# A planner that writes a kernel's order learns when each transfer's eighth predecessor ends

## The chip, the cores and the metric

One core of a Trainium2 chip runs the whole kernel in one launch. The metric is the device time of one execution in microseconds (us); every kernel is run several times and the median is quoted.

## The reference, cut to what matters

One decoder layer for a prompt of 1024 tokens and 64 sample tokens (8 sequences of 8), d_model 1024, all in fp32:

```
h = rmsnorm(x) * norm1_g ;  proj = h @ w_in                      # one input projection
y_conv = c_b * conv3(c_c * c_x)                                  # short gated convolution
r,k,v,decay,a,g from the other columns (token shift, low-rank products)
for each token: s = s*decay - (s@kk) (kk*a)^T + v k^T ; y = s@r   # 8 heads of 64
y_rwkv = (groupnorm(y) + bonus) * g
x = x + [y_conv, y_rwkv] @ w_out                                 # output projection
x = x + relu(rmsnorm(x) @ w_ff1)^2 @ w_ff2 ; y = rmsnorm(x)
```

Outputs are y for both kinds of tokens and the new convolution, shift and recurrent states.

## The kernel before

**Matmuls.** Each fp32 operand is split into a high and a low part, and a product is three matmuls (hi*hi, lo*hi, hi*lo). The 1088 tokens are cut into groups of 384, 384 and 320.

**The recurrence.** The 8 heads are taken as 4 pairs, and a pair with a token group is a *unit* (12 units, 0 to 11, three of a pair in a row). Inside a unit the delta rule goes in chunks: within a chunk it is solved with a triangular inverse, from chunk to chunk a state is handed on. This hand-over is the *chain*: 64 steps in all. One step is L1110, L1111 and L1114 on PE (into `rc`), the copy `X` on DVE (L1120), L1122 on PE, `UT` on ACT (L1124), L1126 on PE, then `Gh` on DVE (L1130 or L1132) and `GD` on ACT (L1116), with which the next step's L1114 begins. L1110 and L1111 don't depend on the step before. A unit's result is read out by `py` (L1144) and transposed by `pty` (L1293). Ahead of a unit lie its inverse on POOL (L1040, L1042), the merge of its blocks (`pz` L1074, copies `wz`, `pz` L1082, `Tt` L1086), the transposes `ptk` (L977, copied to `KT` by ACT at L981) and `ptv` (L992, to `VT` at L997), and the bonus `pb` (L953, L954). In the last unit but one, unit 10, chain steps 55 to 60 run; unit 9 has steps 49 to 54.

**The filler.** The matmuls of the input projection (L664, helper `mm_s`) and then of the output projection (L671, helper `mm_m`) need no chain and are laid between the chain's instructions. Their weights come as 256 KB loads `wraw` (L640), issued by ACT except for the first four, and are split by ACT into `whi` (L652) and by DVE into `wlo` (L654).

**Who sets the order.** All streams (chain, inverse, merge, projections, loads, row loads) are Python generators. Before each group of instructions a generator yields `ck(engine, cost, ...)`, with what it needs (`deps`, tiles `acq`). `Weave.run` (from L312) keeps an estimated clock for each engine, always takes the group that can start earliest, and lets its generator emit its instructions. So what the kernel contains is fixed, and the estimated clocks decide only in which order each engine gets it. The engines work through that order one by one; the clocks and costs of the planner exist nowhere on the chip.

**Transfers.** SP and ACT issue them. In the program every transfer is given one of eight semaphores in turn, over both queues, and its issue waits until the transfer eight before it, which had the same semaphore, has ended. The planner before knows nothing of this. The row loads `mr` (`load_row`, L1321) are issued by ACT; they bring rows of the mixed activations for the output projection.

After some 710 us the woven half ends and plain loops follow: the MLP's first product (L103), its second (L1547, L1559) and the final norm.

Of the kernel before, what the change touches and what calls it, by code (L numbers as in the profile page):

```python
# [33 lines left out]
def tile_kernel(ctx: ExitStack, tc: tile.TileContext, io: dict):  # L34
# [105 lines left out]
    def gen_vec():  # L140
# [4 lines left out]
        for nm, ap, n in VECS:  # L145
            SP.dma_start(vr[off[nm]:off[nm] + n, :], ap.rearrange("(m p) -> m p", p=128))
# [13 lines left out]
        SP.dma_start(ssr, io["state_shift"][0].rearrange("b (m p) -> (b m) p", p=128))  # L160
        SP.dma_start(scr, io["state_conv"][0].rearrange("b j (m p) -> (b j m) p", p=128))
# [20 lines left out]
    def gen_masks():  # L182
# [39 lines left out]
        SP.dma_start(unit_d, winit)  # L222
# [39 lines left out]
    class Weave:  # L262
# [41 lines left out]
        def dma(self, kb=192):  # L304

            t = self.charge("SP", 0.5)
            self.clk["DMA"] = max(self.clk["DMA"], t + 0.65) + kb / 360
            return self.clk["DMA"] + 1.05

        def run(self, gens):  # L310

            st = [[0.0, next(g, None), "PE"] for g in gens]  # L312
            while any(a is not None for _, a, _ in st):
                best, held = None, set()
                for i, (r, a, pe) in enumerate(st):
# [10 lines left out]
                    if held.intersection(acq):  # L326
# [3 lines left out]
                            + [self.credits[t][acq.count(t) - 1] + 0.2 for t in acq])  # L330
# [23 lines left out]
    def ck(eng, cost, **o):  # L354
        return eng, cost, o

# [65 lines left out]
    def load_xt(t):  # L422
        s, n = TOK[t]
        xts[t] = p0.tile([128, D], F32, tag="xt", name="xt", bufs=4)
        SP.dma_start(xts[t][:n], tok_rows(io["x_prompt"], io["x_sample"], t))
# [20 lines left out]
    def gen_lora_w():  # L446
        for nm in ("w2", "a2", "g2"):
            yield ck("SP", 1.2 if nm != "g2" else 0.6, deps=[("n1", 2)])
            raw = p0.tile([128, RW], F32, tag="lraw", name="lraw", bufs=2)
            if nm == "g2":  # L450
                SP.dma_start(raw, io[nm][0])
            else:
                SP.dma_start(raw[0:64], io[nm][0])
                SP.dma_start(raw[64:128], io[nm][0])
# [44 lines left out]
    def gen_lora(parts):  # L499

        for p in range(4):
            for g in range(3):
                s, n = GROUPS[g]
                pc = slice(128 * p, 128 * p + 128)
                for nm in parts:
# [22 lines left out]
                    SP.dma_start(dst[pc, s:s + n], t[:, :n])  # L528
# [63 lines left out]
    def post_conv_b(j, g):  # L592
        def f(acc):
# [5 lines left out]
            def store():  # L599
                SP.dma_start(mix_d[128 * j:128 * j + 128, s:s + n], cc[:, s:s + n])  # L600
# [30 lines left out]
    def gen_load(loads):  # L631

        for x, ld in enumerate(loads):
            for i, (pl, t, src) in enumerate(ld.parts):
                if x < 2:
                    yield ck("NO", 0, acq=("wra" + t,))
                else:
                    yield ck("ACT", 0.05, lat=0, acq=("wra" + t,))
                raw = pl["pq"].tile(list(src.shape), F32, tag="wraw" + t, name="wraw", bufs=2)
                (SP if x < 2 else A).dma_start(raw, src)  # L640
# [145 lines left out]
    def load_sgta(u):  # L786
# [4 lines left out]
        SP.dma_start(sg[:, :n], sig_d[pc, s:s + n])  # L791
        ta = at["pe"].tile([128, 384], F32, tag="ta", name="ta")
        SP.dma_start(ta[:, :n], ta_d[pc, s:s + n])
# [32 lines left out]
    def gen_ew(u):  # L826
# [91 lines left out]
        yield ck("SP", 1.9)  # L918
# [3 lines left out]
        for h in range(2):  # L922
            for i in range(2):
                r = 64 * h + 32 * i
                SP.dma_start(lv[h, i], LT[r:r + 32, :nch, 32 * i:32 * i + 32])
# [39 lines left out]
    def gen_tokens(u):  # L965
# [34 lines left out]
        if g == 2:  # L1000
            yield ck("SP", 0.5, nb=True, deps=[("So", p - 1, 4)] if p else [])
            e["Sn"] = Sn = at["pp"].tile([128, NB, 64], F32, tag="Sn", name="Sn")
            SP.dma_start(Sn, io["state_wkv"][0, :, 2 * p:2 * p + 2].rearrange("b h v k -> (h v) b k"))
# [5 lines left out]
    def load_W(u):  # L1009
        Ws[u] = at["pp"].tile([96, 8, 32], F32, tag="W", name="W", bufs=2)  # L1010
        SP.dma_start(Ws[u], unit_d)
        wv.mark(("W", u), wv.dma(96))

    def gen_invert(u):
# [8 lines left out]
        yield ck("SP", 1.6, lat=4.3, deps=[("A", u)])  # L1023
        M, lt_d = at["M"], e["lt_d"]
        for i in range(4):
            SP.dma_start(M[24 * i:24 * i + nb], lt_d[:nb])
# [18 lines left out]
        yield ck("SP", 1.8)  # L1045
        w_d = dp.tile([24, 32, 32], F32, tag="w_d", name="w_d", bufs=3)
        for q in range(4):
            SP.dma_start(w_d[:nb].rearrange("b (m q) t -> q b m t", q=4)[q], W[24 * q:24 * q + nb])
# [3 lines left out]
    def gen_merge(u):  # L1052
# [5 lines left out]
        yield ck("SP", 1.8, lat=6.5, deps=[("w_d", u)] + done(u - 2))  # L1058
# [5 lines left out]
        for h in range(2):  # L1064
            for i in range(2):
                SP.dma_start(Tt[Q[h][i], :nch, Q[h][i]], wv_[h, i])
# [25 lines left out]
    def gen_recur(u):  # L1092
# [53 lines left out]
        if g == 2:  # L1146
# [8 lines left out]
            SP.dma_start(io["new_wkv_p"][0, 0, 2 * p:2 * p + 2].rearrange("h v k -> (h v) k"), So)  # L1155
# [6 lines left out]
    def gen_sample(u):  # L1162
# [3 lines left out]
        def store_s(So, b0):  # L1166
            for b in range(4):
                SP.dma_start(io["new_wkv_s"][0, b0 + b, 2 * p:2 * p + 2].rearrange("h v k -> v h k"),
# [82 lines left out]
    def load_gt(u):  # L1251
# [3 lines left out]
        SP.dma_start(gts[u][:, :n], gate_d[128 * p:128 * p + 128, s:s + n])  # L1255
        wv.dma()

    def gen_finish(u):
# [42 lines left out]
        if p < 3:  # L1301
            def store():
                SP.dma_start(mix_d[512 + 128 * p:640 + 128 * p, s:s + n], gt[:, :n])
# [56 lines left out]
    def load_x(pl, t):  # L1360
        n = TOK[t][1]
        x1[t] = pl.tile([128, D], F32, tag="x1", name="x1", bufs=6 if t < 6 else 3)
        SP.dma_start(x1[t][:n], tok_rows(io["x_prompt"], io["x_sample"], t))
# [68 lines left out]
    def gen_states():  # L1432
# [12 lines left out]
        SP.dma_start(io["new_shift_p"][0, 0].rearrange("(m p) -> m p", p=128), ns[0:14])  # L1445
        SP.dma_start(io["new_shift_s"][0].rearrange("b (m p) -> (b m) p", p=128), ns[14:126])
        SP.dma_start(io["new_conv_p"][0, 0].rearrange("j (m p) -> (j m) p", p=128), ncv[0:8])
        SP.dma_start(io["new_conv_s"][0].rearrange("b j (m p) -> (b j m) p", p=128), ncv[8:72])
# [13 lines left out]
    with tc.manual_schedule():  # L1462
# [3 lines left out]
        SP.dma_start(g1, io["norm1_g"][0].rearrange("(o n) -> o n", o=1))  # L1466
# [63 lines left out]
    def load_f2(ft):  # L1530
        raw = p5.tile([128, D], F32, tag="f2r", name="f2r", bufs=2)
        SP.dma_start(raw, io["w_ff2"][0][128 * ft:128 * ft + 128, :])
# [62 lines left out]
    def final_c(t, pool_too=True):  # L1595
# [11 lines left out]
        SP.dma_start(tok_rows(io["y_prompt"], io["y_sample"], t), out[:n])  # L1607
# [14 lines left out]
    with tc.manual_schedule():  # L1622
# [27 lines left out]
        SP.dma_start(tok_rows(io["y_prompt"], io["y_sample"], seq[-2]), out)  # L1650
# [3 lines left out]
        SP.dma_start(tok_rows(io["y_prompt"], io["y_sample"], last), xg)  # L1654
# [27 lines left out]
```

## Time and profile before

| | |
|---|---|
| runs | 1471.01, 1471.39, 1469.06 us, median 1471.01 |
| profiled execution | 1467.82 us, its span 1466.1 us |
| mean granted TensorE clock | 0.985 of full |
| PE busy | 1428.1 us, 97% |
| ACT busy, DVE busy, POOL busy | 508.4, 823.6, 317.4 us |
| DMA | 108.25 MB, mean 74 GB/s |

The span is the time from the first to the last instruction of the profiled execution; 1.7 us of that execution lie around it. A timeline row gives the start, the duration, the engine (ACTq and SPq are the queues' issuing instructions), the line, the tiles and, in brackets, how long the engine had been idle before and what ended it. Rows of equal form that follow each other are merged (x2, x4), and the duration is then that of all of them.

### The profile page before, as it was taken

To read this page: it belongs to the slowest core of one execution; us is meant where nothing else is said; L and a number is where in the kernel's file an instruction comes from. 1 tells how busy PE (TensorE), PEld (TensorE's weight loads), DVE (VectorE), ACT (ScalarE), POOL (GpSimd) and SP (SyncE) were. 2 spreads that over 40 slices of the span, in tenths; PEclk is the share of its full clock that TensorE was granted. 3 is DMA by queue.
4 is the path that set the end of the run, shared out by engine and by line. 5 is a ranking of instruction groups with operands and counts; after the bars stand their busy time and mean duration, and the time that the engine had idled before them with its cause. 6 is when DMAs were issued, how large, how long until landed. Compare 5 with 4: busy or idle time off the path is not lost.

```text
span 1466.1 us, 25883 instructions
## 1 busy us (share of the span) xinstructions
PE 1428.1 (97%) x10163; PEld 1339.9 (91%) x10163; DVE 823.6 (56%) x1788; ACT 508.4 (35%) x1094; POOL 317.4 (22%) x855
## 2 busy tenths in 40 slices
PE   6999999999989997999999999999999999999997
PEld 5999999998989987999999999999999999999996
DVE  6537767787767785666444344444344344444347
ACT  6532334344333432344522332223322332223315
POOL 4011656654665655000000000000000000000004
PEclk8999999999989998999999999999999999999999
DMA  6242332232232325453210111111111111111103
GB/s 193 94 146 87 80 84 69 66 91 57 72 85 57 74 74 184 149 171 101 87 44 29 58 58 44 42 31 59 44 43 30 58 58 44 42 32 58 36 1 122
DMA packets 140228, 108.25 MB, mean 74 GB/s; under 512 B 43837, under 2 KB 131017, under 8 KB 140106
## 3 DMA queue, kind: packets, MB, share of 16 engines
q1 hardware_dynamic: 65322, 61.29, 14.0%
q10 hardware_dynamic: 74784, 45.30, 10.5%
q8 instruction: 80, 1.31, 0.4%
q14 instruction: 42, 0.34, 0.1%
HBM read 88.46 MB, written 18.09 MB: 73 GB/s over the span
## 4 chain that ended last, share of the span: by engine, by line
PE 87%; DVE 5%; DMA 3%; POOL 2%; issue 1%; ACT 1%; SPq 0%; ACTq 0%; POOLq 0%; DVEq 0%
PE acc L103 24%; PE acc L664 21%; PE acc L1547 17%; PE acc L1559 8%; PE acc L671 6%; DMA mr<-mix_d 1%; PE pm L899 1%; PE py L1144 1%; PE pw L516 1%; PE rc L1122 1%; DMA wraw<-in_w_out 1%; PE rc L1111 1%; PE pt L403 1%; POOL wtmp L1040 1%; POOL W L1042 1%
## 5 line engine op out<-in xcount | busy, mean ns | idle before, releaser
L103 PE MATMUL acc<-h_lo,whi 128*128 128x320 f32 (+1 forms) x720 | 234.8, 326 | 0.0
L103 PE MATMUL acc<-h_hi,wlo 128*128 128x320 f32 (+1 forms) x720 | 234.8, 326 | 0.0
L103 PE MATMUL acc<-h_hi,whi 128*128 128x320 f32 (+1 forms) x720 | 234.7, 326 | 0.0
L664 PE MATMUL acc<-h_hi,whi 128*128 128x384 f32 (+1 forms) x672 | 230.5, 343 | 2.8 <-DVE nsT L259 2.8
L664 PE MATMUL acc<-h_lo,whi 128*128 128x384 f32 (+1 forms) x672 | 229.4, 341 | 1.6 <-DVE h_lo L414 1.6
L664 PE MATMUL acc<-h_hi,wlo 128*128 128x384 f32 (+1 forms) x672 | 229.9, 342 | 0.0
L1549 DVE TENSOR_TENSOR x<-acc,x 128x512 f32<-128x512 f32 (+1 forms) x193 | 132.8, 688 | 124.9 <-PE acc L1547 124.9
L1593 POOL TENSOR_TENSOR rsf<-rsf,nhalf 128x1 f32<-128x1 f32 (+1 forms) x9 | 8.0, 888 | 741.5 <-DVE rsf L1590 740.4
L1425 DVE TENSOR_TENSOR slo<-r,shi 128x384 fp32r<-128x384 f32 (+1 forms) x96 | 51.5, 537 | 204.5 <-ACT shi L1423 204.5
L1040 POOL TENSOR_TENSOR wtmp<-W,gM 96x60 f32<-96x60 f32 (+24 forms) x372 | 122.3, 329 | 155.3 <-DMA gM<-lt_d 71.3
L1547 PE MATMUL acc<-f2h,shi 128*128 128x512 f32 (+1 forms) x386 | 150.2, 389 | 0.0
L1547 PE MATMUL acc<-f2h,slo 128*128 128x512 f32 (+1 forms) x386 | 150.0, 389 | 0.0
L1547 PE MATMUL acc<-f2l,shi 128*128 128x512 f32 (+1 forms) x386 | 149.9, 388 | 0.0
L68 ACT CAST f2h<-f2r 128x1024 fp32r<-128x1024 f32 x32 | 32.0, 1047 | 309.1 <-PE acc L1547 309.1
L103 PEld LDWEIGHTS acc<-h_lo,whi 128*128 128x128 f32 x720 | 135.1, 188 | 0.6
L103 PEld LDWEIGHTS acc<-h_hi,whi 128*128 128x128 f32 x720 | 135.1, 188 | 0.6
L103 PEld LDWEIGHTS acc<-h_hi,wlo 128*128 128x128 f32 x720 | 135.2, 188 | 0.0
L664 PEld LDWEIGHTS acc<-h_hi,whi 128*128 128x128 f32 x672 | 128.6, 191 | 4.5 <-ACT KT L981 3.0
L1042 POOL TENSOR_TENSOR W<-W,wtmp 96x60 f32<-96x60 f32 (+24 forms) x372 | 126.3, 340 | 29.2
L664 PEld LDWEIGHTS acc<-h_lo,whi 128*128 128x128 f32 x672 | 128.7, 191 | 2.7 <-DVE h_lo L414 1.9
L664 PEld LDWEIGHTS acc<-h_hi,wlo 128*128 128x128 f32 x672 | 128.6, 191 | 0.4
L1419 ACT ACTIVATE r<-acc 128x384 f32<-128x384 f32 (+1 forms) x96 | 45.3, 472 | 150.9 <-PE acc L103 141.2
(308 smaller groups left out, 2833.2 us busy)
## 6 DMA issues: line engine op xcount, KB each, us to landing
f2r<-in_w_ff SPq DMA_DIRECT2D x32, 512.0 KB
wraw<-in_w_ff ACTq DMA_DIRECT2D x64, 256.0 KB
wraw<-in_w_in ACTq DMA_DIRECT2D x48, 256.0 KB
wraw<-in_w_out ACTq DMA_DIRECT2D x48, 256.0 KB
xt<-in_x_prompt SPq DMA_DIRECT2D x8, 512.0 KB
x<-in_x_prompt SPq DMA_DIRECT2D x8, 512.0 KB
out_y_prompt<-out SPq DMA_DIRECT2D x7, 512.0 KB
gM<-lt_d SPq DMA_DIRECT2D x32, 96.0 KB
```

Of the source, the lines that this page charges most:

```text
L68: A.copy(hi, src)
L103: PE.matmul(acc[:, :n], a, b, start=(i == 0), stop=(i == 23))
L403: PE.transpose(pt[:, k, :n], xn[:n, 128 * kk:128 * kk + 128], ident[:n, :n])
L664: PE.matmul(acc[:, :n], a, b, start=(k == i == 0), stop=(k == 7 and i == 2))
L671: PE.matmul(acc[:n, :256], a, b, start=(k == i == 0), stop=(k == 7 and i == 2))
L1040: G.tensor_tensor(tv, W[:, 0:nr, r:r + 1].broadcast_to([96, nr, wd]), M[:, r:r + 1, r + 1:32].broadcast_to([96, nr, wd]), op=ALU.mult)
L1042: G.tensor_tensor(W[:, 0:nr, r + 1:32], W[:, 0:nr, r + 1:32], tv, op=ALU.subtract)
L1419: A.activation(r[:, :n], acc[:, :n], AF.Relu)
L1425: V.tensor_tensor(lo, r[:, :n], hi.bitcast(F32), op=ALU.subtract)
L1547: PE.matmul(acc[:, :cn], a, b, start=(j == 0), stop=(j == 3 * FB - 1))
L1549: V.tensor_tensor(x1[t][:, cols], acc[:, :cn], x1[t][:, cols], op=ALU.add)
L1559: PE.matmul(acc[:, :n], a, b, start=(j == 0), stop=(j == 3 * FB - 1))
```

## The change

The planner gets a list `lanes` of the expected end of every transfer so far, eight zeros at first. Each issue of the woven half goes through `sp_dma` or `act_dma`, which appends an expected end of 2.2 us after the planner's now, SP's clock (for SP) or the eighth predecessor's expected end, whichever is last. `dma` and `dma_a`, where the program calls them behind an issue, put their own estimate in its place, and `dma` lets SP's clock wait for the eighth predecessor. A group marked `dma=k` may not start before the expected end of the eighth predecessor of its k-th transfer, plus 0.3 us. Marked are the weight loads on ACT (k=1) and the groups of four small transfers on SP (k=4): stores of `lt_d` and `w_d`, loads of `gM` and `Tt`. The row loads `mr` are counted in the list and are not marked.

```diff
 class Weave:
+            self.lanes = [0.0] * 8
...
         def dma_a(self, kb=192):
             self.clk["DMA"] = max(self.clk["DMA"], self.now + 0.65) + kb / 360
-            return self.clk["DMA"] + 1.05
+            self.lanes[-1] = self.clk["DMA"] + 1.05
+            return self.lanes[-1]
...
         def dma(self, kb=192):
-            t = self.charge("SP", 0.5)
+            t = self.charge("SP", 0.5, self.lanes[-9])
             self.clk["DMA"] = max(self.clk["DMA"], t + 0.65) + kb / 360
-            return self.clk["DMA"] + 1.05
+            self.lanes[-1] = self.clk["DMA"] + 1.05
+            return self.lanes[-1]
...
                     t = max([r + (0.05 if eng == "PE" and pe != "PE" else 0), self.clk[eng]]
                             + [self.done[k] + 0.2 for k in o.get("deps", ())]
-                            + [self.credits[t][acq.count(t) - 1] + 0.2 for t in acq])
+                            + [self.credits[t][acq.count(t) - 1] + 0.2 for t in acq]
+                            + ([self.lanes[o["dma"] - 9] + 0.3] if "dma" in o else []))
...
+    def sp_dma(out, src, **kw):
+        wv.lanes.append(max(wv.now, wv.clk["SP"], wv.lanes[-8]) + 2.2)
+        SP.dma_start(out, src, **kw)
+
+    def act_dma(out, src, **kw):
+        wv.lanes.append(max(wv.now, wv.lanes[-8]) + 2.2)
+        A.dma_start(out, src, **kw)
...
-                    yield ck("ACT", 0.05, lat=0, acq=("wra" + t,))
+                    yield ck("ACT", 0.05, lat=0, acq=("wra" + t,), dma=1)
...
-        yield ck("SP", 1.9)
+        yield ck("SP", 1.9, dma=4)
...
-        yield ck("SP", 1.8, lat=6.5, deps=[("w_d", u)] + done(u - 2))
+        yield ck("SP", 1.8, lat=6.5, deps=[("w_d", u)] + done(u - 2), dma=4)
...
     def load_row(raw, g, k):
         s, n = GROUPS[g]
-        A.dma_start(raw[:, :n], mix_d[128 * k:128 * k + 128, s:s + n])
+        act_dma(raw[:, :n], mix_d[128 * k:128 * k + 128, s:s + n])
```

The `gM` loads and `w_d` stores are marked in the same way, and all other issues of the woven half are only renamed. Both programs hold the same instructions on every engine. In the changed one the lines stand 12 lower from L358 on (L664 is L676, L671 is L683, L1122 is L1134, L1126 is L1138), and issues by ACT show the helper's line, L367.

Three places show what moves. The first is PE where the input projection ends. Rows with `acc` are filler, rows with `rc` are the chain, `pm` belongs to unit 11. Before, from the last half of step 56:

```order
L1126 MATMUL rc<-UT,KT_1292 128x64
L664 MATMUL acc<-h_lo,whi 128x320
L664 MATMUL acc<-h_hi,wlo 128x320
L671 MATMUL acc<-whi,h_hi 128x256
L671 MATMUL acc<-wlo,h_hi 128x256
L671 MATMUL acc<-whi,h_lo 128x256
L671 MATMUL acc<-whi,h_hi 128x256
L1110 MATMUL rc<-VT,KT_1292 128x64
L1111 MATMUL rc<-VT,AMK_1290 128x64
L1114 MATMUL rc<-Gh,AR_1287 128x64
L671 MATMUL acc<-wlo,h_hi 128x256
L671 MATMUL acc<-whi,h_lo 128x256
```

And changed, from the last matmul of the input projection:

```order
L676 MATMUL acc<-h_hi,wlo 128x320
L1134 MATMUL rc<-X,Tt_1309 128x64
L1138 MATMUL rc<-UT,KT_1317 128x64
L1122 MATMUL rc<-VT,KT_1317 128x64
L1123 MATMUL rc<-VT,AMK_1313 128x64
L1126 MATMUL rc<-Gh,AR_1310 128x64
L1134 MATMUL rc<-X,Tt_1309 128x64
L911 MATMUL pm<-AR_1312,KB 128x128 x2
L1138 MATMUL rc<-UT,KT_1317 128x64
L1122 MATMUL rc<-VT,KT_1317 128x64
L1123 MATMUL rc<-VT,AMK_1313 128x64
L1126 MATMUL rc<-Gh,AR_1310 128x64
```

The last matmul of the input projection is followed by steps 57 to 60 in the kernel before, and by the second half of step 52 and all of 53 to 60 in the changed one.

The second place is PE a little later, from the last output-projection matmul that can run before a third part of its weights is there. `pts` and `pxs` are the sample tokens' pieces, `pty` and `pb` transposes and the bonus. Before:

```order
L671 MATMUL acc<-whi,h_lo 128x256
L1126 MATMUL rc<-UT,KT_1292 128x64
L1181 MATMUL pts<-ident,Sn 64x64 x8
L1110 MATMUL rc<-VT,KT_1292 128x64
L1111 MATMUL rc<-VT,AMK_1290 128x64
L1114 MATMUL rc<-Gh,AR_1287 128x64
L1181 MATMUL pts<-ident,Sn 64x64 x8
L953 MATMUL pb<-rk_hi,bonesr 128x320
L954 MATMUL pb<-rk_lo,bonesr 128x320
L1122 MATMUL rc<-X,Tt_1284 128x64
L1195 MATMUL pxs<-AR_1288,G_7577 64x2x8 x8
```

And changed:

```order
L683 MATMUL acc<-whi,h_lo 128x256
L1138 MATMUL rc<-UT,KT_1316 128x64
L1122 MATMUL rc<-VT,KT_1316 128x64
L1123 MATMUL rc<-VT,AMK_1314 128x64
L1126 MATMUL rc<-Gh,AR_1311 128x64
L1134 MATMUL rc<-X,Tt_1308 128x64
L1138 MATMUL rc<-UT,KT_1316 128x64
L1122 MATMUL rc<-VT,KT_1316 128x64
L1123 MATMUL rc<-VT,AMK_1314 128x64
L1126 MATMUL rc<-Gh,AR_1311 128x64
L1305 MATMUL pty<-ident,yn 128x128 x3
L1134 MATMUL rc<-X,Tt_1308 128x64
```

Before, the last matmul of the filler stands between the two halves of step 57; changed, between the two halves of step 56.

The third is ACT, where the six row loads are issued in one go. `GD` and `UT` are the chain's, `KT`, `VT`, `rk_hi` and `Tt` are what unit 10 needs. Before, from step 54's `UT`:

```order
L1124 ACTIVATE UT<-rc,nneg 128x64
L981 COPY KT_1293<-ptk 64x3x64 x4
L1275 ACTIVATE ysq<-yc 128x384
L549 CAST h_hi<-cc 128x384
L981 COPY KT_1293<-ptk 64x2x64 x4
L1321 DMA mr<-mix_d 128x384 x6
L997 COPY VT<-ptv 64x192
L947 CAST rk_hi<-kp 128x320
L1086 ACTIVATE Tt_1284<-pz 32x6x32 x2
```

And changed, from step 53's `UT` (L1136):

```order
L1136 ACTIVATE UT<-rc,nneg 128x64
L1128 ACTIVATE GD<-Gh,dc 128x64
L1136 ACTIVATE UT<-rc,nneg 128x64
L367 DMA mr<-mix_d 128x384 x6
L959 CAST rk_hi<-kp 128x320
L993 COPY KT_1317<-ptk 64x3x64 x4
L561 CAST h_hi<-mr 128x384
L993 COPY KT_1317<-ptk 64x2x64
L1287 ACTIVATE ysq<-yc 128x384
L1098 ACTIVATE Tt_1308<-pz 32x6x32 x2
L993 COPY KT_1317<-ptk 64x2x64 x2
```

Before, the row loads stand behind the eight `KT` copies of unit 10 and ahead of its `VT`, `rk_hi` and `Tt`; changed, they stand directly behind step 54's `UT`, ahead of all of these.

## Rows read from the trace of the kernel before

**Rows 1.** The page, busy time: engine, us, share of span, instructions.

```profile
PE 1428.1 (97%) x10163; PEld 1339.9 (91%) x10163; DVE 823.6 (56%) x1788; ACT 508.4 (35%) x1094; POOL 317.4 (22%) x855
```

**Rows 2.** The page, the chain that ended last, by engine.

```profile
PE 87%; DVE 5%; DMA 3%; POOL 2%; issue 1%; ACT 1%; SPq 0%; ACTq 0%; POOLq 0%; DVEq 0%
```

**Rows 3.** Windows: stretch, length, busy PE, PEld, DVE, ACT, POOL, granted clock, DMA share, GB/s.

```profile
431.49:445.14 13.65, 12.34 (x92) 10.96 (x93) 7.70 (x25) 4.64 (x16) 11.08 (x33) 0.50 0.17 51
550.24:571.38 21.14, 14.57 (x140) 13.28 (x140) 11.48 (x27) 6.29 (x16) 17.22 (x51) 0.84 0.54 176
```

**Rows 4.** Timeline of PE, last input-projection matmul and the chain steps behind it: start, duration.

```profile
550.24 0.31 PE L664 MATMUL acc<-h_hi,wlo 128*128 128x320 f32 x1
...
550.50 0.28 PE L671 MATMUL acc<-wlo,h_hi 128*128 128x256 f32 x1
550.62 0.28 PE L671 MATMUL acc<-whi,h_lo 128*128 128x256 f32 x1
...
553.20 0.43 PE L1126 MATMUL rc<-UT,KT 128*128 128x64 f32 x2
...
557.55 0.43 PE L1126 MATMUL rc<-UT,KT 128*128 128x64 f32 x2
...
559.68 0.43 PE L1122 MATMUL rc<-X,Tt 128*128 128x64 f32 x2 [0.32 <-DVE X L1120]
...
563.96 0.69 PE L1126 MATMUL rc<-UT,KT 128*128 128x64 f32 x2 [3.84 <-ACT UT L1124]
...
571.38 0.47 PE L1126 MATMUL rc<-UT,KT 128*128 128x64 f32 x2
```

**Rows 5.** Timeline of ACT and its queue, in the same stretch and before it.

```profile
539.99 3.36 ACTq L1321 DMA_DIRECT2D mr<-mix_d  x3
...
556.88 2.00 ACTq L640 DMA_DIRECT2D wraw<-in_w_out  x4
...
558.92 3.87 ACTq L1321 DMA_DIRECT2D mr<-mix_d  x2
...
562.84 0.35 ACT L1116 ACTIVATE GD<-Gh,dc 128x64 f32<-128x64 f32 x1 [5.66 <-DMA wraw<-in_w_out]
```

**Rows 6.** Timeline, the links of a chain step.

```profile
424.35 0.33 PE L1122 MATMUL rc<-X,Tt 128*128 128x64 f32 x2
...
425.08 0.43 PE L1126 MATMUL rc<-UT,KT 128*128 128x64 f32 x2 [0.40 <-ACT UT L1124]
...
558.02 0.28 DVE L1132 SCALAR_TENSOR_TENSOR Gh<-rc,dc,GD 128x64 f32<-128x64 f32 x1 [0.70 <-PE rc L1126]
...
558.98 0.39 PE L1114 MATMUL rc<-Gh,AR 128*128 128x64 f32 x2
...
559.40 0.23 DVE L1120 COPY X<-rc 128x64 f32<-128x64 f32 x1 [0.51 <-PE rc L1114]
```

**Rows 7.** Timeline, reading out one unit and preparing the next.

```profile
426.04 0.33 PE L1144 MATMUL py<-VT,AMK 64*64 64x64 f32 x4
...
428.17 0.45 PE L953 MATMUL pb<-rk_hi,bonesr 128*128 128x384 f32 x1
...
432.80 0.66 PE L664 MATMUL acc<-h_hi,whi 128*128 128x384 f32 x1 [2.80 <-DVE nsT L259]
...
434.67 0.85 PE L1074 MATMUL pz<-wz,LT 32*32 32x32 f32 x24
...
543.97 0.65 ACT L1086 ACTIVATE Tt<-pz 32x192 f32<-32x192 f32 x2
```

**Rows 8.** Groups of instructions, PE from 36 to 710 us: count, busy us, mean ns.

```profile
L977 PE MATMUL ptk<-ident,KB 128*128 128x128 f32 x68 | 11.7, 277 | 0.5 <-DVE bv L958 0.5
```

**Rows 9.** Timeline of PE, the first half of a chain step under other work.

```profile
479.19 0.33 PE L1110 MATMUL rc<-VT,KT 128*128 128x64 f32 x2
...
479.78 0.39 PE L664 MATMUL acc<-h_lo,whi 128*128 128x320 f32 x1
```

**Rows 10.** The weight cast L652: what ended ACT's idle time before it: us, times.

```profile
  DMA wraw<-in_w_out: 1.0, 2
```

More of the change, by code (lines that the diff above doesn't have):

```diff
@@ L221, in gen_masks @@
         yield ck("SP", 0.5)
-        SP.dma_start(unit_d, winit)
+        sp_dma(unit_d, winit)
         yield ck("ACT", 0.2)
@@ L450, in gen_lora_w @@
             if nm == "g2":
-                SP.dma_start(raw, io[nm][0])
+                sp_dma(raw, io[nm][0])
             else:
-                SP.dma_start(raw[0:64], io[nm][0])
-                SP.dma_start(raw[64:128], io[nm][0])
+                sp_dma(raw[0:64], io[nm][0])
+                sp_dma(raw[64:128], io[nm][0])
             hi = p0.tile([128, RW], F32R, name=nm + "h")
@@ L637, in gen_load @@
                 else:
-                    yield ck("ACT", 0.05, lat=0, acq=("wra" + t,))
+                    yield ck("ACT", 0.05, lat=0, acq=("wra" + t,), dma=1)
                 raw = pl["pq"].tile(list(src.shape), F32, tag="wraw" + t, name="wraw", bufs=2)
-                (SP if x < 2 else A).dma_start(raw, src)
+                (sp_dma if x < 2 else act_dma)(raw, src)
                 ld.raw.append(raw)
@@ L790, in load_sgta @@
         sg = at["pe"].tile([128, 384], F32, tag="sg", name="sg")
-        SP.dma_start(sg[:, :n], sig_d[pc, s:s + n])
+        sp_dma(sg[:, :n], sig_d[pc, s:s + n])
         ta = at["pe"].tile([128, 384], F32, tag="ta", name="ta")
-        SP.dma_start(ta[:, :n], ta_d[pc, s:s + n])
+        sp_dma(ta[:, :n], ta_d[pc, s:s + n])
         sgta[u] = sg, ta
@@ L1010, in load_W @@
         Ws[u] = at["pp"].tile([96, 8, 32], F32, tag="W", name="W", bufs=2)
-        SP.dma_start(Ws[u], unit_d)
+        sp_dma(Ws[u], unit_d)
         wv.mark(("W", u), wv.dma(96))
@@ L1022, in gen_invert @@
             load_W(0)
-        yield ck("SP", 1.6, lat=4.3, deps=[("A", u)])
+        yield ck("SP", 1.6, lat=4.3, deps=[("A", u)], dma=4)
         M, lt_d = at["M"], e["lt_d"]
         for i in range(4):
-            SP.dma_start(M[24 * i:24 * i + nb], lt_d[:nb])
+            sp_dma(M[24 * i:24 * i + nb], lt_d[:nb])
         wv.mark(("M", u), wv.now + 2.3)
@@ L1065, in gen_merge @@
             for i in range(2):
-                SP.dma_start(Tt[Q[h][i], :nch, Q[h][i]], wv_[h, i])
+                sp_dma(Tt[Q[h][i], :nch, Q[h][i]], wv_[h, i])
         for h in range(2):
@@ L1444, in gen_states @@
         yield ck("SP", 2.0)
[L1445 to L1448, printed above, removed]
+        sp_dma(io["new_shift_p"][0, 0].rearrange("(m p) -> m p", p=128), ns[0:14])
+        sp_dma(io["new_shift_s"][0].rearrange("b (m p) -> (b m) p", p=128), ns[14:126])
+        sp_dma(io["new_conv_p"][0, 0].rearrange("j (m p) -> (j m) p", p=128), ncv[0:8])
+        sp_dma(io["new_conv_s"][0].rearrange("b j (m p) -> (b j m) p", p=128), ncv[8:72])
         wv.mark("states")
@@ L1465, in tile_kernel @@
         G.memset(ones, 1.0)
-        SP.dma_start(g1, io["norm1_g"][0].rearrange("(o n) -> o n", o=1))
+        sp_dma(g1, io["norm1_g"][0].rearrange("(o n) -> o n", o=1))
         wv.dma(4)
@@ L1653, in tile_kernel @@
         V.scalar_tensor_tensor(xg[:, 512:], x1[last][:, 512:], rs, gF[:, 512:], op0=ALU.mult, op1=ALU.mult)
-        SP.dma_start(tok_rows(io["y_prompt"], io["y_sample"], last), xg)
+        sp_dma(tok_rows(io["y_prompt"], io["y_sample"], last), xg)
 _INS = ["x_prompt", "x_sample", "state_conv", "state_shift", "state_wkv", "norm1_g", "w_in", "conv_w", "mu",
```

40 lines of the change are left out of this document (20 added, 20 removed).

## Prediction

> **What bounds the kernel now.** The page's busy times come first: PE works 97% of the span, the next engine 56% [rows 1], and the chain that ended last lies on PE for 87% [rows 2]. So time is lost or won only where PE idles or runs at half clock, and nothing else that is moved counts unless PE comes to wait for it. The windows say where that is. From 550.24 to 571.38 it is busy 14.57 of 21.14 us, and from 431.49 to 445.14 its granted clock is 0.50 [rows 3], which is the lower of its two levels, 1.2 GHz. These two places hold most of what an order can change. The second half, plain loops, is the same in both programs.
>
> The timeline shows why. Around 430 us PE had no filler and stood still for 2.80 us until the copy nsT of the token shift was done [rows 7]; the half clock follows that stop. Behind 550.24 the input projection is over, the output projection has only two parts of its weights, and the last steps of the chain stand nearly bare: they end (L1126) at 553.20, 557.55, 563.96 and 571.38 [rows 4]. The worst wait there is 3.84 us at 563.96, for UT. ACT, which makes UT, issued four weight loads and two row loads; the row loads' issue took 3.87 us, and GD, the next thing on ACT, began 5.66 us after ACT's work before it, with a weight load as its releaser [rows 5]. So an issue whose predecessor on its semaphore still runs does hold up what stands behind it on the engine. That is what the planner is now told of.
>
> **The change part by part.** Nothing is added or removed on the chip: the sum is made of orders alone.
>
> *The gates on loads and small transfers.* The marked loads move by at most some 18 filler matmuls in the order. One is paid only if the cast of the weights waits for it, and in the whole trace the casts waited for output-projection loads twice, 1.0 us in all [rows 10], though they come in time for matmuls over 50 places later. I cost this at 0; the cover is those 50 matmuls. Bounds: a gain of the 1.0 us, a loss of 3 us if three casts come late by a us each.
>
> *The row loads.* They are not marked, and the two that made the 3.84 us wait stay where they were, ahead of step 60's GD and UT. That wait I keep. The six issued earlier together, whose last three took 3.36 us [rows 5], are now ahead of KT, Tt and VT of unit 10 instead of VT and Tt; PE waited about a us for VT then. I cost the move at 0, with bounds -1 (that wait is gone) and +3.4 (all of the issue time falls on unit 10's start).
>
> *The chain against the filler.* This is the main effect and the order shows it. With several groups held back in the estimate, the chain falls behind the filler: what had steps 57 to 60 left when the input projection ended now has half of step 52 and steps 53 to 60 left, with unit 9's py and unit 10's whole preparation. Of output-projection matmuls 31 stood ahead of step 60's end, now 12. The sum, from the last L664 to step 60's L1126:
> - Price of a bare step. A floor: L1126 to Gh 0.47, Gh 0.28, L1114 to X 0.42, X to L1122 0.28, L1122 to L1126 0.73 [rows 4, 6], together 2.2 us. The bare part at 557.55 to 559.68 took 2.13 and with 0.73 for the rest of the step 2.86. With sample pieces in between a step took 4.35 (553.20 to 557.55). I take 3.1, nearest to the 2.86, since most of the eight whole steps have little in between. 8 x 3.1 = 24.8, and 0.9 for the half step.
> - Between units 9 and 10: pb about 0.6, py 426.04 to 428.17 = 2.1, five ptk at 0.17 (11.7 us over 68) = 0.9, two pz passes at about 0.5 (0.85 at half clock), Tt 0.65 and the copy wz about as long [rows 7, 8]: 5.9, of which 2.2 is already in the step that goes on: 3.7.
> - The ACT wait: 3.84 [rows 4].
> - Together 33.2 us, where the kernel before took 21.1 [rows 4]: +12.1.
> - Against this, work that stood ahead of the last L664 now lies behind it, so that L664 ends earlier: 4.5 steps, of which L1110, L1111 and L1114 take 0.59 [rows 9] and L1122 and L1126, two of such five pairs, 0.4, so 4.5; py 2.1; pz 1.0; ptk and as many ptv 1.8: -9.4.
> - 19 output-projection matmuls are still to be done, at 0.12 each by their spacing [rows 4]: +2.3.
> - Half clock. A pair L1126 takes 0.69 us at 563.96, at half clock, and 0.43 at full [rows 4], so the 0.9 us of matmul in a step becomes 1.45. If four of the eight steps fall into it: +2.2.
>
> Sum: 12.1 - 9.4 + 2.3 + 2.2 = +7.2 us. With the floor of 2.2 for a step it is 0.0, without half clock -2.2; with 4.35, and the clock low for all eight, +19.
>
> *The stop at 430 us.* Its pieces (py, pty, ptk without filler, and an acc behind the token shift) come together again in the changed order, 144 filler matmuls later, again with nothing between them; by the same rows their chain of waits is about 7.5 us over 4.5 us of matmuls. I cost it at 0. Bounds: if it is gone, 2.80 us of idle and what the half clock costs; the 12.34 busy us of that window [rows 3] would be some 7.7 at full clock by the ratio 0.43 to 0.69 above, so 4.6 more, 7.4 in all; +3 if it is longer.
>
> *The head.* The projections' casts and the token transposes change places there by a few instructions; 0, with 3 us either way.
>
> The profiled execution took 1467.82 us; plus 7.2 is 1475.0. The runs' median, 1471.0, is 3.2 higher, and so I predict **1478.2 us**.
>
> A rule that bears on the main term is in the Trainium skill, DMA: Bandwidth & Descriptors, section Anatomy of one DMA: a transfer costs about 2.0 us fixed plus its bytes over 436 thousand per us, which makes an estimate of 2.6 us for 256 KB, near the planner's 2.2. It is measured for a path that another engine issues, and the trace here speaks against it for loads that share the wires: the loads issued from 556.88 on still held an issue until 562.79, over five us later [rows 5]. By the page the gate would look far enough ahead and the ACT wait would shrink by some 3 us, to +4 in all.
>
> **The rivals.**
> 1. *Faster: the stop at 430 is dissolved.* The chain now comes later against the filler there, and it takes only some ten more L664 between py and the token shift to fill 2.80 us and keep the clock up. Price -7.4 at the most; it decides as soon as the end of the input projection costs less than that, which needs bare steps at 2.86 or below and little half clock: 7.2 - 1.9 - 2.2 - 7.4 = -4.3, 1466.7 us. For it: PE's clock is low after that one stop. Against it: the order holds no filler there.
> 2. *No change: the bare steps cost what the moved work saves.* At 2.2 to 2.4 us a step and full clock the end costs -2.2 to -0.6, some 1469.6 us. For it: PE waited only 0.32 us at 559.68 in a nearly bare step [rows 4]. Against it: nothing in that stretch ran at the floor.
> 3. *Slower still: bare steps at 4.35 and half clock throughout, or the six row loads in front of unit 10.* +13 to +19, some 1487 us. For it: the granted clock falls after stops, and nine nearly bare steps are a long one.
> 4. *Slower by late weights.* The Trainium skill, DMA: Bandwidth & Descriptors, Rules for kernel authors, says that a DMA should be issued early and waited for late, which speaks against holding any back. In this kernel it would show as casts that wait for wraw, each with a us of PE. The row of the casts [rows 10] and 50 matmuls of reserve speak against it: five late casts would give +5 on top, 1483 us.
> 5. *The change doesn't do what it says:* row loads aren't gated, so the issue that held ACT before is there again. That is in my sum.
>
> **How the numbers follow.** A difference of 0.2%, 2.9 us, is about what a measurement of this kernel can tell from none. Forecast (slower by 3 to 13 us): 0.52; rival 3, 0.10; rival 4, 0.03: slower 0.65. Rival 2: 0.16. Rival 1: 0.19. The forecast's own range is 1474 to 1484. To hold 8 in 10 it reaches down to the bulk of rival 1 and up to the first half of rival 3: 1466 to 1488.
>
> **What would show it.** Right: in the changed profile PE is idle for some 12 us or more between the last L676 (was L664) and step 60's L1138, with a dozen UT and X waits of 0.5 to 1.5 us; the granted clock in that stretch is under 0.8; a wait for UT of about 4 us with ACT's row loads ahead of it; and the stop for nsT still there some 20 us later than before. The second half takes as long as it did. Wrong: no stop for nsT and full clock from 430 to 460 us; or step intervals of 2.2 to 2.4 us at the end; or casts waiting for wraw in many places.

## The result

The changed kernel took 1479.34 us (median of 5, 1477.58 to 1483.84), the kernel before 1469.06 us on the same chip (5 runs): ratio 1.0074, 95% interval 1.0051 to 1.0097, so some 10 us slower. The forecast was 1478.2 us in a range of 1466 to 1488, with slower as the likeliest case.

The profiled execution of the changed kernel is the slowest of its five, 1483.84 us with a span of 1482.1; a second trace, taken with the experiments, has a span of 1478.8. What the two don't share is named below. The kernel before was traced at 1467.82 us, so the two traced pairs differ by 16.0 and 12.7 us, more than the medians do.

### The profile after

The page first. Busy times have the same shape as before [rows 1]; PE's busy time is 11.8 us longer with the same instructions:

```profile
PE 1439.9 (97%) x10163; PEld 1351.1 (91%) x10163; DVE 824.3 (56%) x1788; ACT 508.0 (34%) x1094; POOL 316.8 (21%) x855
```

More busy time for the same work is work at a lower clock. The windows view (stretch, length, busy PE, PEld, DVE, ACT, POOL, granted clock, DMA share, GB/s) shows the woven half behind its head, then, behind the head's own, the stretches in it in which the clock was at 0.50, 1.2 GHz, throughout:

```profile
36.50:738.51 702.01, 682.35 (x5942) 644.66 (x5942) 470.54 (x1216) 267.94 (x640) 283.77 (x799) 0.96 0.33 95
332.54:335.95 3.41, 3.30 (x13) 3.11 (x13) 1.36 (x4) 2.16 (x6) 2.78 (x10) 0.50 0.08 22
475.90:482.72 6.82, 5.64 (x41) 4.75 (x40) 5.93 (x22) 2.96 (x8) 5.57 (x17) 0.50 0.24 67
540.75:547.58 6.83, 6.43 (x61) 5.23 (x62) 5.66 (x19) 1.12 (x3) 0.00 (x0) 0.50 0.52 130
554.41:557.82 3.41, 3.41 (x18) 3.37 (x18) 2.09 (x6) 2.48 (x7) 2.75 (x9) 0.50 0.14 30
561.23:585.12 23.89, 19.03 (x179) 17.11 (x179) 9.42 (x22) 4.88 (x12) 13.27 (x45) 0.50 0.52 174
612.43:619.26 6.83, 6.67 (x32) 6.67 (x32) 2.23 (x6) 2.77 (x8) 0.00 (x0) 0.50 0.16 48
```

Before, the same half (36.50 to 722.76) is 686.26 us long with PE busy 670.23:

```profile
36.50:722.76 686.26, 670.23 (x5942) 633.17 (x5942) 468.38 (x1212) 268.28 (x640) 285.29 (x798) 0.98 0.34 97
```

So PE idled 16.0 us in this half before and 19.7 us after: 3.6 us of the 15.8 that the half grew. Most of the rest is the clock. A filler matmul of 384 columns starts 0.32 us before the next at half clock, and 0.17 to 0.18 us before it at full clock. The kernel before shows both:

```profile
423.99 0.34 PE L664 MATMUL acc<-h_lo,whi 128*128 128x384 f32 x1
424.17 0.34 PE L664 MATMUL acc<-h_hi,wlo 128*128 128x384 f32 x1
...
440.42 0.52 PE L664 MATMUL acc<-h_hi,whi 128*128 128x384 f32 x1
440.74 0.52 PE L664 MATMUL acc<-h_lo,whi 128*128 128x384 f32 x1
```

So I count 0.45 of the busy time at half clock as lost; this factor is an estimate from these rows. The rows at 0.50 hold 44.5 busy us. With 5.4 us at half clock in the head they are 49.9, a loss of 22.4; before it was 25.7 busy us, a loss of 11.6. That is 10.8 of the 15.8. In the second trace the half grew by 12.4 us: idle time by 3.4, the clock's loss by 6.8.

Where is it lost? The timeline of PE from the last matmul of the input projection on, with the ends of the chain's steps 52, 53, 54, 55, 56 and 60 (L1138 was L1126):

```profile
535.75 0.31 PE L676 MATMUL acc<-h_hi,wlo 128*128 128x320 f32 x1
...
536.86 0.43 PE L1138 MATMUL rc<-UT,KT 128*128 128x64 f32 x2 [0.40 <-ACT UT L1136]
...
540.27 0.43 PE L1138 MATMUL rc<-UT,KT 128*128 128x64 f32 x2
...
543.78 0.69 PE L1138 MATMUL rc<-UT,KT 128*128 128x64 f32 x2 [0.40 <-ACT UT L1136]
...
554.18 0.51 PE L1138 MATMUL rc<-UT,KT 128*128 128x64 f32 x2 [0.59 <-ACT UT L1136]
...
558.61 0.43 PE L1138 MATMUL rc<-UT,KT 128*128 128x64 f32 x2 [0.23 <-ACT UT L1136]
...
578.92 0.69 PE L1138 MATMUL rc<-UT,KT 128*128 128x64 f32 x2 [4.15 <-ACT UT L1136]
```

The windows view of this stretch:

```profile
535.75:578.92 43.17, 33.99 (x300) 28.55 (x299) 23.95 (x66) 14.37 (x43) 21.33 (x64) 0.68 0.41 119
```

From the last L676 to step 60 it is 43.2 us where the kernel before took 21.1 [rows 4]. The wait for UT is there again, 4.15 us for 3.84, and ACT's timeline shows the same cause, four weight loads and two row loads, and the six row loads at step 54:

```profile
543.42 3.21 ACTq L367 DMA_DIRECT2D mr<-mix_d  x6
546.82 0.46 ACT L959 CAST rk_hi<-kp 128x320 fp32r<-128x320 f32 x1 [3.09 <-DMA mr<-mix_d]
...
570.90 2.05 ACTq L367 DMA_DIRECT2D wraw<-in_w_out  x4
572.99 4.76 ACTq L367 DMA_DIRECT2D mr<-mix_d  x2
577.80 0.35 ACT L1128 ACTIVATE GD<-Gh,dc 128x64 f32<-128x64 f32 x1 [6.60 <-DMA wraw<-in_w_out]
```

GD waited 6.60 us; before it was 5.66 [rows 5]. The wait that the planner was taught to see is no shorter; the row loads that meet it are counted in the list but not marked. The stop at 430 us [rows 7] moved to 473 us and became two, 1.08 and 1.18 us, with 6.8 us of half clock behind in place of 13.65 (3.4 in the second trace):

```profile
474.55 0.55 PE L989 MATMUL ptk<-ident,KB 128*128 128x128 f32 x3 [1.08 <-ACT KT L993]
...
477.52 0.69 PE L676 MATMUL acc<-h_hi,whi 128*128 128x384 f32 x1 [1.18 <-ACT cc L576]
```

### The profile page after: what moved, and what is told of

Same layout as the page of the kernel before. It is cut to its first block, busy times and chain, and to the rows that moved or that the text cites. A ratio compares the mean times of both kernels' runs of the same rounds, so it can differ in the third digit from the quotient of the medians.

```text
span 1482.1 us, 25870 instructions
## 1 busy us (share of the span) xinstructions
PE 1439.9 (97%) x10163; PEld 1351.1 (91%) x10163; DVE 824.3 (56%) x1788; ACT 508.0 (34%) x1094; POOL 316.8 (21%) x855
## 4 chain that ended last, share of the span: by engine, by line
PE 91%; DVE 5%; DMA 2%; ACT 1%; issue 1%; POOL 1%; POOLq 0%; ACTq 0%; DVEq 0%
PE acc L103 24%; PE acc L676 22%; PE acc L1559 17%; PE acc L1571 8%; PE acc L683 6%; PE py L1156 2%; PE pm L911 1%; PE rc L1138 1%; DMA wraw<-in_w_out 1%; PE rc L1134 1%; PE pw L528 1%; PE rc L1123 1%; PE rc L1126 1%; PE rc L1122 1%; PE pt L415 1%
## 5 line engine op out<-in xcount | busy, mean ns | idle before, releaser
L676 PE MATMUL acc<-h_hi,whi 128*128 128x384 f32 (+1 forms) x672 | 229.3, 341 | 2.7 <-DVE X L1132 1.4
L676 PE MATMUL acc<-h_lo,whi 128*128 128x384 f32 (+1 forms) x672 | 228.1, 339 | 1.5 <-DVE rs L63 1.5
L676 PE MATMUL acc<-h_hi,wlo 128*128 128x384 f32 (+1 forms) x672 | 229.1, 341 | 0.0
L676 PEld LDWEIGHTS acc<-h_hi,whi 128*128 128x128 f32 x672 | 128.3, 191 | 4.4 <-ACT Tt L1098 1.6
L676 PEld LDWEIGHTS acc<-h_lo,whi 128*128 128x128 f32 x672 | 128.2, 191 | 2.4 <-DVE rs L63 1.8
L676 PEld LDWEIGHTS acc<-h_hi,wlo 128*128 128x128 f32 x672 | 128.2, 191 | 1.0
```

What stands on the lines that cost most here:

```text
L676: PE.matmul(acc[:, :n], a, b, start=(k == i == 0), stop=(k == 7 and i == 2))
```

## The experiments

Theory A: the change lets the chain fall behind the filler, and the loss is where the chain then lies bare, that is, without filler between its steps. Theory B: transfers that are held back arrive late. Theory C, within A: most of it is the half clock that a thin stretch brings.

All runs stand in one table. The ratio (with its interval) is to the kernel before on the same chip, whose median there was 1468.5 to 1469.8 us. Then come, from each trace, from 36.5 us to the first matmul of the MLP, PE's idle time, its busy time at half clock, and what is left of the length when idle time and 0.45 of that busy time are taken off.

| kernel | median us | ratio | idle | busy at half | rest |
|---|---|---|---|---|---|
| before (trace of 1467.82) | 1471.01 | | 16.0 | 25.7 | 658.7 |
| changed | 1479.34 | 1.0074 (1.0051 to 1.0097) | 19.7 | 49.9 | 659.9 |
| changed, second trace | 1480.40 | 1.0077 (1.0053 to 1.0101) | 19.4 | 40.7 | 660.9 |
| only_charge | 1481.73 | 1.0067 (1.0040 to 1.0094) | 21.6 | 43.8 | 658.6 |
| only_small | 1502.18 | 1.0212 (1.0173 to 1.0250) | 30.1 | 72.2 | 658.9 |
| only_weights | 1469.65 | 0.9991 (0.9966 to 1.0016) | 16.2 | 28.2 | 657.2 |
| no_charge | 1502.41 | 1.0219 (1.0182 to 1.0255) | 30.7 | 67.0 | 660.1 |
| before_l2 | 1499.46 | 1.0202 (1.0155 to 1.0249) | 25.9 | 58.6 | 660.4 |
| before_late52 | 1492.37 | 1.0169 (1.0144 to 1.0194) | 28.4 | 53.7 | 659.5 |
| before_late55 | 1474.98 | 1.0025 (0.9995 to 1.0055) | 20.8 | 32.6 | 658.8 |
| after_rows_sp | 1480.18 | 1.0094 (1.0061 to 1.0128) | 17.7 | 41.5 | 660.4 |
| before_rows_sp | 1461.87 | 0.9948 (0.9927 to 0.9970) | 13.0 | 21.1 | 656.6 |
| rows_sp_x | 1466.56 | 0.9989 (0.9973 to 1.0005) | 13.7 | 28.5 | 657.0 |
| after_junk | 1486.16 | 1.0128 (1.0104 to 1.0152) | 16.3 | 49.9 | 668.0 |

The rest is the same within some 4 us in all kernels that hold the same instructions, while their half is from 679 to 721 us long. So the orders differ in the main by idle time and half clock; effects of one to four us lie within what this account leaves open. A straight line through the 13 traces with the same instructions gives a loss of 0.50 per busy us at half clock, near the 0.45. This is an account and no proof of which came first: the thin stretches are both those in which PE idles and those in which the clock is low.

Where each kernel loses is worth a second table: idle time and 0.45 of the busy time at half clock together, for three parts of the half.

| kernel | up to the last input-projection matmul | from there to step 60 | behind step 60 |
|---|---|---|---|
| before | 16.2 | 8.4 | 3.0 |
| changed | 12.9 | 19.4 | 9.8 |
| changed, second trace | 12.2 | 19.3 | 6.3 |
| only_charge | 10.1 | 16.7 | 14.5 |
| only_small | 32.8 | 12.7 | 17.0 |
| before_l2 | 29.4 | 11.3 | 11.5 |
| before_late52 | 20.0 | 17.5 | 15.1 |
| before_late55 | 17.9 | 10.2 | 7.3 |

In the changed kernel 11 us more are lost in the bare end, 3 to 4 less ahead of it, and 3 to 7 more behind it, where unit 11's steps follow. only_charge and before_late52 lose 8 and 9 us more in the bare end and 12 more behind it. only_small and before_l2 lose most of theirs ahead of the end, so they don't tell what the bare end costs.

### Which part of the change does it

**only_charge**: no gates, SP's clock alone.

```diff
-                    yield ck("ACT", 0.05, lat=0, acq=("wra" + t,), dma=1)
+                    yield ck("ACT", 0.05, lat=0, acq=("wra" + t,))
-        yield ck("SP", 1.9, dma=4)
+        yield ck("SP", 1.9)
```

(the other three dma=4 likewise)

> Only the planner's SP clock waits for the eighth predecessor; no group is held back by a gate. Its order leaves steps 52 to 60 of the chain behind the last matmul of the input projection, as the whole change does. Theory A (the time follows the number of chain steps left bare there): about +10 us over the kernel before, 1.005 to 1.010 of it, and as in the changed kernel a stretch of 40 us or more from the last L676 to step 60's L1138. Theory B (held-back transfers arrive late): no gate, no loss, within 3 us of the kernel before.

1.0067: without a single gate nearly the whole loss is there, and from the last L676 to step 60 it is 41.6 us. So theory B doesn't explain the change. The rows of that stretch's ends:

```profile
530.24 0.31 PE L676 MATMUL acc<-h_hi,wlo 128*128 128x320 f32 x1
...
571.87 0.66 PE L1138 MATMUL rc<-UT,KT 128*128 128x64 f32 x2
```

**only_weights**: the weight gate alone (all dma=4 taken out, `self.charge("SP", 0.5)` as before).

> Only the weight loads on ACT are gated; SP's clock and its groups are as before. The chain's steps stand against the filler exactly as in the kernel before, with a few instructions changed elsewhere. Theory A: same time as before, within 2.5 us. Theory B (held-back loads arrive late): slower by 3 us or more, with casts of the weights waiting for wraw.

0.9991, no difference that can be told: the gate on weight loads alone costs nothing and gains nothing, as forecast.

**only_small**: the four dma=4 alone (dma=1 and the charge taken out).

> Only the groups of four small transfers on SP are gated; weights and SP's clock are not. Seven steps (54 to 60) lie behind the last matmul of the input projection, six of them with no filler at all. Theory A: less than the whole change, +5 to +9 us over the kernel before. Theory B: the gates are the whole loss, +10 us or more, and waits for gM, w_d or Tt show on POOL or DVE.

1.0212, three times the whole change: more than theory A allowed, while theory B set no upper limit. Theory B's signs hardly show. POOL waited less for gM and for w_d than in the kernel before (59.9 and 14.0 us for 71.3 and 36.6), and the one merge that came late is unit 11's: PE waited 3.98 us for DVE's wz at 600 us. In its trace a weight load on ACT could not be issued, and UT behind it kept PE waiting for 7.36 us:

```profile
204.08 0.53 ACT L246 ACTIVATE xr<-acc,omu 128x320 f32<-128x320 f32 x1 [1.38 <-PE acc L676]
211.98 0.38 ACTq L367 DMA_DIRECT2D wraw<-in_w_in  x1
212.41 0.62 ACT L664 CAST whi<-wraw 128x512 fp32r<-128x512 f32 x1 [7.80 <-DMA w_d<-W]
```

SP's queue in the same stretch:

```profile
209.81 3.27 SPq L363 DMA_DIRECT2D w_d<-W  x4
```

The load's eighth predecessor was the first of these w_d stores, which SP issued only at 209.81; both tell their end on the same semaphore. Besides, a whole unit's chain lay bare at 422 to 450 us, with 30.7 us of half clock from 425 to 463. So the count of bare steps behind the last L676, which theory A had named, is not enough: the filler can leave the chain bare in other places too.

**no_charge**: both gates, without the charge.

```diff
-            t = self.charge("SP", 0.5, self.lanes[-9])
+            t = self.charge("SP", 0.5)
```

> Both kinds of gate, but SP's clock in the plan doesn't wait for the eighth predecessor. Against the kernel with the gates on small transfers alone the weight loads are gated too. If that gate does its work, the 7.4 us for which ACT's weight load waited at 204.6 us for a w_d store that SP had not issued yet is gone or small, and the time is 4 to 12 us below that kernel's: 1490 to 1498 us. Rival: the order still leaves that load where it was: within 3 us of 1502 us.

1502.41: the rival. PE's wait for UT is 5.45 us in place of 7.36, the store still the releaser:

```profile
209.71 0.62 ACT L664 CAST whi<-wraw 128x512 fp32r<-128x512 f32 x1 [5.88 <-DMA w_d<-W]
```

The weight gate is meant for just this case and didn't remove it. I take it that the expected end of such a store, 2.2 us after the planner's now, is too early for one that waits for POOL; that was not tried.

### Is it what the planner is told, or the order that comes out

**before_l2**: the opposite advice, transfers planned shorter, no lanes.

```diff
-        yield ck("SP", 1.6, lat=4.3, deps=[("A", u)])
+        yield ck("SP", 1.6, lat=4.0, deps=[("A", u)])
-        yield ck("NO", 0, lat=2.5)
+        yield ck("NO", 0, lat=2.2)
-        yield ck("SP", 1.8, lat=6.5, deps=[("w_d", u)] + done(u - 2))
+        yield ck("SP", 1.8, lat=6.0, deps=[("w_d", u)] + done(u - 2))
```

> The kernel before, with the planner's waits behind the small transfers made shorter by 0.3 to 0.5 us (4.0, 2.2 and 6.0 for 4.3, 2.5 and 6.5): the opposite of what the change tells the planner. Its order too leaves steps 52 to 60 behind the last matmul of the input projection. Theory A: slower than before by 8 to 12 us, like the change. Theory B: transfers are planned earlier, so same or faster than before.

1.0202. Told that transfers are quicker, the planner also leaves steps 52 to 60 behind the input projection, and the kernel is slower still, above either theory's range, with stops where a merge came before its data (PE's waits: us in total, times, the longest):

```profile
PE pz L1074 <- DVE wz L1069: 6.1, 6, 2.6
PE acc L671 <- ACT whi L652: 4.7, 2, 2.8
PE rc L1126 <- ACT UT L1124: 4.7, 8, 1.6
```

So it isn't the sense of the correction: two settings away from that of the kernel before, in opposite directions, both lost. But they lost in different places. Of the 25 us that idle time and clock took here beyond the kernel before, 13.2 lie ahead of the last input-projection matmul, 2.9 in the bare end and 8.5 behind it. So this run doesn't speak for theory A.

**before_late52** and **before_late55**: the order of the kernel before up to there, then the chain held.

```diff
-            yield ck("PE", 0.45, gap=0.02, acq=("rec",), lat=0.2 if first else 0, deps=[("T", u), ("B", u)] + done(u - 1) if c == 0 else [])
+            yield ck("PE", 0.45, gap=0.02, acq=("rec",), lat=0.2 if first else 0, deps=[("T", u), ("B", u)] + done(u - 1) if c == 0 else [("acc", nmain - 1)] if (u, c) == (9, 3) else [])
```

(late55: `[("acc", nmain - 1)]` is added where u is 10 and c is 0.)

> The kernel before, its order the same up to step 51; from step 52 on the chain is held in the plan until the last matmul of the input projection is out, so that steps 52 to 60 lie bare as in the changed kernel. No lanes, no gates. Theory A (the bare end of the chain is the loss): +7 to +14 us over the kernel before, with 40 us or more from the last L664 to step 60's L1126. Rival (the loss of the change is spread over the first 530 us and the end only shows it): within 3 us of before.

> The kernel before, its order the same up to step 54; only unit 10 (steps 55 to 60) is held until the last matmul of the input projection is out. Four steps lay behind it before, six do now. Theory A with the measured rates: 2 more steps at some 3.9 us less their PE work, some half clock more, +4 to +10 us, well under the 24 us of the kernel that holds from step 52 on. Rival (the time doesn't follow the number of bare steps): within 3 us of before, or as slow as from step 52 on.

From step 52 on: 1.0169, some 24 us, more than the range given. From 55 on: 1.0025, on the side of theory A, but its interval takes in no difference. Theory A's direction holds and the loss grows with what is held, but not in proportion. In late52 it is 37 us from the last L664 to step 60 (544.61 to 581.64), under the 40 expected. 4.43 us of that is one wait of PE, for a merge of unit 10; the changed kernel has 0.65 there. More than the end itself, what lies behind it cost: unit 11 came late too and stood bare:

```profile
549.97 0.85 PE L1082 MATMUL pz<-Tt,wz 32*32 32x32 f32 x24 [4.43 <-DVE wz L1078]
...
592.05 1.10 PE L1074 MATMUL pz<-wz,LT 32*32 32x32 f32 x20 [3.98 <-DVE wz L1069]
```

### The clock, and the row loads

**after_junk**: extra matmuls in the bare steps.

```diff
+    def junk(u, c, rc):
+        if u == 10 or (u == 9 and c > 2):
+            for _ in range(4):
+                PE.matmul(rc[:, 192:320], bonesr, bonesr, start=False, stop=True, skip_group_check=True)
```

It is called ahead of X and behind L1134: eight a step, 72 in all, not twelve a step as the expectation has it.

> The changed kernel with twelve short extra matmuls in each of steps 52 to 60 (four after L1126 of the first part, four after L1134, four before L1122's X), about 0.7 us of added PE work a step in its idle time, into a free part of the same PSUM tile. Theory C (most of the loss is the half clock that the thin stretch brings): the granted clock between 536 and 586 us rises from 0.5 to 0.7 to above 0.9 except behind the 4 us wait, and the time falls by 4 to 8 us against the changed kernel. Rival (the links of the chain are the loss): the clock rises or not, the time is the same or up to 4 us longer.

1.0128, some 7 us slower than the changed kernel: theory C's gain didn't come, and it is more than the 4 us that the rival allowed. The clock in the stretch stayed low (0.69 from 536 to 586, PE busy 44.61 of 50). Idle time fell by 3.4 us and the table's rest grew by 8.1, which I put down to the added work:

```profile
536.00:586.00 50.00, 44.61 (x378) 39.54 (x378) 24.35 (x68) 14.31 (x43) 22.18 (x65) 0.69 0.37 106
```

Theory C is not refuted by this run, since the clock didn't rise, and not shown either. How much would be left of the loss at full clock stays open.

**after_rows_sp** and **before_rows_sp**: row loads issued by SP. The edit to the kernel before; in the changed one the load is still counted in the list, with the estimate of `act_dma`.

```diff
     def load_row(raw, g, k):
-        A.dma_start(raw[:, :n], mix_d[128 * k:128 * k + 128, s:s + n])
+        SP.dma_start(raw[:, :n], mix_d[128 * k:128 * k + 128, s:s + n])
```

> The changed kernel with the row loads mr issued by SP, at the same places in the order. Theory: the 4.15 us wait for UT goes, with the 3 us that ACT stood still at step 54, and 4 to 8 us fall away against the changed kernel; what stays is the bare end, so it is still 2 to 6 us slower than the kernel before. Rival: the wait only passes to the casts of the weights: within 3 us of the changed kernel.

> The kernel before with the row loads mr issued by SP in place of ACT, at the same place in the order. Theory: ACT no longer stands behind an issue that waits for its semaphore; the 3.84 us wait of PE for UT before step 59's L1126 falls under 1 us and the half clock behind it with it: -3 to -6 us. Rival: SP has x loads to issue at the same time and waits for their semaphores itself, the rows come later and PE waits for h_hi of the rows instead: within 2 us of before.

On the kernel before: 0.9948, faster by some 7 us and the fastest of these kernels. On the changed kernel there was no gain, as its rival had it. In both the wait for UT only shrank, to 3.02 and 2.82 us, since UT now stood behind a cast of weights that waited for its load:

```profile
561.53 0.62 ACT L652 CAST whi<-wraw 128x512 fp32r<-128x512 f32 x1 [2.85 <-DMA wraw<-in_w_out]
562.06 0.31 ACT L1124 ACTIVATE UT<-rc,nneg 128x64 f32<-128x64 f32 x1
```

(These rows are from the kernel before with row loads on SP.) So my reason for the gain holds in small part. Idle time is 3.0 us less in all: 0.8 is that wait, 1.8 the stop before L1122 at 570.34 us in the kernel before, 1.0 a wait for yn at 355, against a new one of 1.7 at 530. Another 2.1 us is half clock. The rest of the account is 2.1 lower, and why stays open.

**rows_sp_x**: as before_rows_sp, and `wv.dma_a(4 * n)` behind each x load in the plan.

> The kernel before with row loads on SP, and the planner's transfer clock also charged with the 512 KB x loads, which it did not know of. The casts of the third part of the output weights are then planned later, behind the chain's UT. Theory: the 3 us wait for UT that was left goes, another -2 to -4 us against row loads on SP alone. Rival: steps 59 and 60 lose their filler (it is planned behind step 60) and that costs as much: the same within 2 us.

0.9989: some 6 us worse than before_rows_sp, where the rival allowed 2. The cast went, and a row's h_hi took its place ahead of GD on ACT and X on DVE:

```profile
561.33 0.43 PE L1114 MATMUL rc<-Gh,AR 128*128 128x64 f32 x2
565.78 0.69 PE L1122 MATMUL rc<-X,Tt 128*128 128x64 f32 x2 [4.02 <-DVE X L1120]
```

**after_again**: the changed kernel once more.

> The changed kernel once more, for a second trace of it. If the account by idle time and half clock is right, the time from the end of the head to the first matmul of the MLP is idle + 0.45 x busy at half clock + a rest of about 659 us, whatever the run. Unit 11's part (the 2.6 us wait for UT at 610 us and the half clock behind it) may or may not be there: with it as in the first profile, without it 3 to 5 us less. Median 1477 to 1482 us.

The account holds within 2 us: 698.7 = 19.4 + 18.3 + 660.9. Of unit 11's loss, in the first trace 2.57 us of waiting for UT at 610 us and 6.8 us of half clock behind it, 0.98 us and no half clock are left. So that loss changes from run to run. The bare end repeats: 43.2 us in both traces, with 9.2 and 9.3 us idle and 22.7 and 22.1 busy us at half clock.

## Why the prediction was right, and where its terms were not

- **Direction and place: right, by the step named.** The chain's fall behind the filler, read from the order, is the loss: the bare end alone took 11 us more of idle time and half clock. only_charge shows that it comes without any gate, before_late52 that holding the chain is enough to lose time, and only_weights that the gate on weight loads alone costs nothing.
- **The sum: its work was sized well, the clock was not.** I compare part by part, in the first trace.
  - Ahead of the last L676 (was L664) the forecast was -9.4 and -14.5 us was measured. By the account 11.2 of that is work that moved behind; 3.3 is idle time and half clock that went, on balance.
  - From there to step 60 the forecast was 33.2 us and 2.2 for half clock, and 43.2 was measured. 22.7 busy us in it were at half clock, a loss of 10.2 by the factor above; without that the stretch is 33.0 us.
  - Behind step 60 the forecast was +2.3, and +8.2 was measured (+5.1 in the second trace). Only 1.4 to 1.8 of that is work; the remainder is idle time and half clock, for which the sum had nothing there.
- **Half clock: the term that failed in size.** "If four of the eight steps fall into it: +2.2", against 10.2 us in that stretch. Idle time, of which I had expected 12 us or more, was 9.2 there, and it grew by only 3.6 in the half. The loss was named as waits and came mostly as clock. That 33.0 meets 33.2 is partly luck: the price of a step, 3.1, measured 3.4, 3.5, 4.4, 2.4, 4.4 and 6.3 from L1138 to L1138, half clock included, with nine filler matmuls in the third and sample pieces in the last two; between unit 9 and 10 it was 10.4 us in place of 6.8.
- **The nearness of 1478.2 to 1479.34 is partly luck.** The forecast stands on 1471.01, while the kernel before had 1469.06 on the same chip, so +7.2 was forecast and +10.3 measured. And the terms missed on both sides.
- **The stop at 430: the 0 was wrong.** It went to 473, 43 us later and not 20, and half of its half clock or more went, with a third of its idle time. Rival 1 came true in part, some 4 us: the 9.2 us of idle time and half clock around it became 5.1. A new stretch of half clock at 332 us took 1.5 of that back.
- **The signs.** Of those named, the clock under 0.8 came (0.68), the wait for UT behind ACT's row loads (4.15 us), and a second half as long as it was (743.6 us for 743.3). The 12 us of idle time and the dozen waits of 0.5 to 1.5 us did not: besides the 4.15 there are 12 waits of over 0.1 us, and only three of them reach 0.5.
- **ACT's wait kept at 3.84: right**, 4.15. The six row loads at 0: right. rk_hi waited 3.09 us for them, but KT had to wait for PE's ptk until 548.95 in any case.
- **Weights at 0: right**, apart from one wait of PE of 1.06 us for wlo at 656.
- **Not seen:** unit 11's wait for UT behind a row's cast, 1.0 to 2.6 us.
- The estimate by the Trainium skill, DMA: Bandwidth & Descriptors, section Anatomy of one DMA (2.6 us for a 256 KB load): the trace disagrees again for loads that run beside each other. The four issued from 570.90 on held an issue until 577.75, and the ACT wait did not shrink by the 3 us that the prediction drew from the page. The same section says that a semaphore wait takes place on the issuing sequencer, ahead of dispatch; the trace agrees, with 4.76 us on ACT's queue and 6.60 us for GD behind it.

## What to carry to other kernels

A planner's estimate is worth what the order that comes out of it is worth. Judge a corrected estimate by where the latency-bound chain lands against its filler, over the whole order and not only at its end: here a correction and its opposite both lost, in different places. Look at whether an engine on the chain issues transfers whose semaphore may still be held. Moving the row loads to another queue gained 0.5% on the kernel before and nothing on the changed one, where modelling the wait lost 0.7%; it took only a fifth and a third off the waits that it was meant to remove. In a thin stretch add up idle time and busy time at half clock together: here the clock's share of the growth was two to three times that of idle time.

## What the runs showed of the hardware that was not expected

An issue can be held by a transfer that has not been issued yet: ACT's weight load stood from 204.6 to 211.98 us for a store that SP sent out at 209.81 (only_small). And in the changed kernel the clock was at half for 23.89 us on end, from 561.23, while PE was busy for 19.03 of them. PE's longest pause in there, 4.15 us, began only at 574.77; up to then none was longer than 0.4 us.
